# A projection started from raw, feature-major activations, and key projections moved into the feed-forward loop

## Chip, cores and metric

The kernel runs on one core of a Trainium2 chip. The metric is the device time of one execution in microseconds. PE is the matmul engine (TensorE), DVE the vector engine, ACT the scalar engine, POOL GpSimd and SP the sync engine, which issues most transfers here.

## What is computed

A network of three stages on 256 tokens of 1024 features, in float32: a block with three attention branches, then two layers with feed-forward parts and a second attention. The change touches the start of the first block and the feed-forward part between the two layers. Cut to that:

```
h = rmsnorm(x, g_mix)                 # x * rsqrt(mean(x*x) + EPS) * g
proj = h @ w_in                       # q, k, v of three branches, index scores, 3072 gate logits
m = rmsnorm(mem, g_mem)
mkv = m @ w_mem_kv                    # keys and values of the memory branch
gates = sigmoid(gate_logits + b_gate)
merged = gates[0]*(o_swa @ wp_swa) + gates[1]*(o_dsa @ wp_dsa) + gates[2]*(o_mem @ wp_mem)
x = x + merged @ w_out
...
kv = h @ kv_w                         # six slots of 4 groups x 64: 0, 1 compressed k and v,
                                      # 2, 3 selected k and v, 4, 5 window k and v
x = post_norm(x, swiglu(x, w1, w3, w2))
...                                   # attention with kv
```

The norm's factor is one number per token, so it can also be applied to a product's rows.

## The kernel before

Every large product is made in three matmuls (`mm3`): each operand is split into a high part, rounded to the matmul's format, and a low part, the rest; high times high, high times low and low times high are summed in PSUM. Activations lie feature-major: 8 tiles `k` of 128 features, each with 256 tokens, once as high part and once as low part (`x = (xh, xl)`). A product is made either with weights as the stationary operand (`up`: the result has features in partitions, 256 tokens as columns) or with activations as the stationary operand (`row`: tokens in partitions).

Weights come through one stream (`Stream`). Each piece of 256 columns is two loads of 512 KB on SP's queue into five rotating raw buffers. ACT casts a load to its high part (`wh`, L142) and DVE subtracts it to get the low part (`wl`, L149). `get` hands out the pieces in the order of the program, and `pump` prepares one ahead. A load waits until the subtraction of the load five places before it has freed its buffer.

The framework's planner orders the instructions of each engine by its own costs and priorities. Inside `manual(...)` the instructions of the named engines keep the order in which they are written, and others may be placed between them. Each engine works through its queue in order.

The first block, `mixers`, begins with `manual(DVE, ACT)`: x is loaded token-major in two row tiles, `rms_rows` makes statistics and the normalised rows, `norm_T` transposes them on PE in 16 pieces of 128x128, applies the gain `g_mix` on the way out of PSUM and splits the result. Gains and biases are loaded as rows (`vectors`) and transposed on PE too. `half` multiplies with the first 452 columns, by halves of the features and by row tiles, into two PSUM banks; L1353 copies the result to `PI`. Then follow two of twelve gate products (`gates`, two ACT copies each with the bias, L1388), rotary embedding of parts of PI on DVE (`rope`), transposes of it (`pair_T`, L597), the projection PQ (`rowproj`), index scores, the norm of memory by the same two functions, the projection PM, further projections by `up`, and three attentions, with the other ten gates and the top-k search (L1474, L1475) woven between them. `merge` applies the sigmoid.

`kv_ffn` runs two value slots by `row`, then slots 0 and 1 (`tokens`), then two key slots (`key`, L1031 and L1034, split by halves of 64 partitions), then a feed-forward part (`ff`) whose first chunk is made by `row` and transposed after swiglu (L535, L536, L497), the other chunks by `up`, with the compression of keys hooked in behind some chunks.

Of the kernel before, what the change touches and what calls it, by code (L numbers as in the profile page):

```python
# [23 lines left out]
F32 = mybir.dt.float32  # L24
# [3 lines left out]
OP = mybir.AluOpType  # L28
AX = mybir.AxisListType

S = 256
# [7 lines left out]
RAW = 5  # L39
LAST = 3  # L40
# [136 lines left out]
class Ker:  # L177
# [60 lines left out]
    def col(self, n, k):  # L238
        g, r = self.vec[n]
        return self.vt[g][:, r + k:r + k + 1]  # L240
# [6 lines left out]

    def vectors(self, names, q):

        nc, I = self.nc, self.I  # L250
        v = self.med([128, 128])
        r = 0
        g = len(self.vt)
        for n in names:
            ap = I[n]
            ap = ap.rearrange({1: "a -> a", 2: "a b -> (a b)", 3: "a b c -> (a b c)"}[len(ap.shape)])
            m = ap.shape[0] // 128
            q.dma_start(v[r:r + m], ap.rearrange("(r p) -> r p", p=128))
            self.vec[n] = (g, r)
            r += m  # L260
        t = self.cp.tile([128, r], F32, name=f"vt{g}")
        self.vt.append(t)

        def put():
            ps = self.bank()
            nc.tensor.transpose(ps[:, :r], v[:r], self.ident[:r, :r])
            nc.scalar.copy(t, ps[:, :r])

        return put
# [87 lines left out]
    def rms_rows(self, xs, ns, part=None, pin=False):  # L357

        nc = self.nc
        mvs = [self.stats(x, D, part, pin) for x in xs]  # L360
# [32 lines left out]

    def norm_T(self, n, t, g, b, x, act=False):

        nc = self.nc
        xh, xl = x
        ts = slice(t * 128, (t + 1) * 128)  # L400
        y = self.med([128, KT, 128])
        for h in range(4):
            ps = self.bank()
            for j in range(2):
                nc.tensor.transpose(ps[:, j * 128:(j + 1) * 128], n[:, (2 * h + j) * 128:(2 * h + j + 1) * 128],
                                    self.ident)
            for j in range(2):
                k = 2 * h + j
                p = ps[:, j * 128:(j + 1) * 128]
                sc = act or h % 2  # L410
                if b is None and sc:
                    nc.scalar.activation(y[:, k], p, AF.Copy, scale=g(k))  # L412
                elif b is None:
                    nc.vector.tensor_scalar(y[:, k], p, g(k), None, op0=OP.mult)
                elif sc:
                    nc.scalar.activation(y[:, k], p, AF.Identity, scale=g(k), bias=b(k))
                else:
                    nc.vector.tensor_scalar(y[:, k], p, g(k), b(k), op0=OP.mult, op1=OP.add)
        for h in range(4):
            ks = slice(2 * h, 2 * h + 2)  # L420
            end = self.split(xh[:, ks, ts], xl[:, ks, ts], y[:, ks])
        return end
# [576 lines left out]
    def kv_ffn(self, x, acc):  # L999
# [38 lines left out]
        def tokens(slot):  # L1038
# [5 lines left out]
            for a in range(2):  # L1044
                p = ps[:, a * S:(a + 1) * S]
                for e in range(2):
                    nc.scalar.copy(T[:64, 2 * a + e], p[half[e]])
                    nc.vector.tensor_copy(T[64:, 2 * a + e, :S - 1], p[half[e], 1:])
# [4 lines left out]
        for b in range(2):  # L1053
            key(b)
# [84 lines left out]
        f = self.ffn(x, 1, 0, acc, {1: keys, 2: lambda: windows(0), 3: lambda: windows(1), 4: compress})  # L1139
# [165 lines left out]
    def mixers(self, p):  # L1305
# [3 lines left out]
        sl = lambda t: slice(t * 128, (t + 1) * 128)  # L1309
        R = self.big([128, 2, D])  # L1310
        self.c, self.vec, self.vt = {}, {}, []
        nc.sync.dma_start(R[:, 0], I["x"][0, :128])
        names = ("ident", "tril_t", "rowok")
        self.load_cst(names, self.cp.tile([128, 257], F32, name="cst"))
        self.ident = self.cst("ident")
        put = [self.vectors(("g_mix", "g_mem"), nc.scalar)]
        nc.sync.dma_start(R[:, 1], I["x"][0, 128:])
        if not self.dry:
            for _ in range(4):
                W.load()  # L1320
# [3 lines left out]
        nr = [self.med([128, D]) for _ in range(2)]  # L1324
        put.append(self.vectors(("b_gate", "cmp_b1_2"), nc.sync))
        x = self.new_xT()
        gm = lambda k: self.col("g_mix", k)
# [3 lines left out]
        def half(ws, j, t):  # L1331
            for i in range(4):
                wh, wl = ws[i // 2]
                k = 4 * j + i
                self.mm3(ps[t][:, :452], x[0][:, k, sl(t)], x[1][:, k, sl(t)], wh[:, i % 2], wl[:, i % 2], k == 0, k == 7)

        with self.manual(mybir.EngineType.DVE, mybir.EngineType.Activation):
            put[0]()
            pw = [W.prep(), W.prep()]
            next(pw[0])  # L1340
            self.rms_rows([R[:, t] for t in range(2)], nr)
            self.norm_T(nr[0], 0, gm, None, x)
            next(pw[0], None)
            ws = W.get(w_in, 0, 4, 1024, 1476, False)
            half(ws, 0, 0)
            self.norm_T(nr[1], 1, gm, None, x)
            next(pw[1])
            next(pw[1], None)
            half(ws, 0, 1)
            ws = W.get(w_in, 512, 4, 1024, 1476, False)  # L1350
# [12 lines left out]
        def rowproj(w, c0, c1, x, P):  # L1363
# [29 lines left out]
        for f in put[1:]:  # L1393
            f()
# [194 lines left out]
```

## Time and profile before

| | us |
|---|---|
| median of 3 timed runs (lowest, highest) | 1489.09 (1487.06, 1489.27) |
| the profiled execution | 1489.02 |
| its span, from the first instruction to the last | 1487.2 |
| PE busy in the span | 1446.4 |
| DVE, ACT, POOL busy | 957.4, 736.1, 40.1 |

The profile is of one execution, and its time stands beside its span. An engine that is not the bottleneck may idle at no cost. Matmuls overlap, each beginning before the last has ended, so the distance between their starts says how fast PE goes, and a wait shorter than the overlap does not show as idle time.

### The profile page before, as it was taken

What the parts mean: (1) busy time and instruction counts of PE and PEld (TensorE: products, weight loads), DVE (VectorE), ACT (ScalarE), POOL (GpSimd) and SP (SyncE); (2) the same over time, 40 slices, a digit from 0 to 9 for tenths busy, and PEclk for the clock granted to TensorE, in tenths of its full rate; (3) what the DMA queues carried; (4) which work ended last, traced back from release to release, by engine and by line L of the source; (5) the groups of instructions that cost most, each with busy time, mean ns of one, the idle gap of its engine ahead of it and who ended that gap; (6) DMA issues with size and microseconds to landing.
All of it is one profiled execution on the core that took longest, in us unless ns stands there. A gap on an engine that the chain in (4) does not pass through costs nothing.

```text
span 1487.2 us, 25225 instructions
## 1 busy us (share of the span) xinstructions
PE 1446.4 (97%) x10093; PEld 1334.0 (90%) x10093; DVE 957.4 (64%) x1630; ACT 736.1 (49%) x1127; POOL 40.1 (3%) x49
## 2 busy tenths in 40 slices
PE   6899999999999999999999999999999999999997
PEld 6699898989999999889899999999999898899996
DVE  7884498555585445886785445866645778664544
ACT  5564565444354444554354444554544397354442
POOL 0000000000000000100010000100000121100001
PEclk9999999999999999999999999999999999999999
DMA  8443166655556665487556665466766452286650
GB/s 278 142 144 106 64 231 239 224 187 183 170 180 197 191 189 180 146 262 258 156 172 200 194 188 180 148 200 218 234 193 184 120 183 86 62 265 185 185 170 29
DMA packets 191714, 264.81 MB, mean 178 GB/s; under 512 B 11024, under 2 KB 159852, under 8 KB 191596
## 3 DMA queue, kind: packets, MB, share of 16 engines
q1 hardware_dynamic: 183068, 249.56, 52.9%
q10 hardware_dynamic: 8528, 13.64, 3.0%
q8 instruction: 79, 1.29, 0.3%
q14 instruction: 39, 0.32, 0.1%
HBM read 262.09 MB, written 1.07 MB: 177 GB/s over the span
## 4 chain that ended last, share of the span: by engine, by line
PE 82%; DVE 10%; ACT 3%; issue 2%; DMA 2%; POOL 0%; ACTq 0%; DVEq 0%; POOLq 0%
PE acc L311 21%; PE u L275 17%; PE u L276 17%; PE u L277 17%; DVE wl L149 3%; PE acc L276 2%; PE acc L695 2%; PE acc L277 2%; PE acc L275 2%; ACT wh L142 1%; DVE big L850 1%; DVE bst L379 1%; PE acc L681 1%; DVE big L828 1%; PE u L799 1%
## 5 line engine op out<-in xcount | busy, mean ns | idle before, releaser
L149 DVE TENSOR_TENSOR wl<-wr,wh 128x1024 fp32r<-128x1024 f32 (+3 forms) x488 | 573.2, 1184 | 419.0 <-ACT wh L142 406.6
L142 ACT CAST wh<-wr 128x1024 fp32r<-128x1024 f32 (+3 forms) x488 | 493.2, 1019 | 531.6 <-PE u L276 226.1
L275 PE MATMUL u<-big,wh 128*128 128x256 f32 x1960 | 552.5, 282 | 1.6 <-ACT med L412 1.1
L277 PE MATMUL u<-big,wl 128*128 128x256 f32 x1960 | 550.3, 281 | 0.0
L276 PE MATMUL u<-big,wh 128*128 128x256 f32 x1960 | 550.3, 281 | 0.0
L275 PEld LDWEIGHTS u<-big,wh 128*128 128x128 f32 x1960 | 369.9, 189 | 4.7 <-ACT med L412 1.3
L276 PEld LDWEIGHTS u<-big,wh 128*128 128x128 f32 x1960 | 369.0, 188 | 2.2
L277 PEld LDWEIGHTS u<-big,wl 128*128 128x128 f32 x1960 | 369.6, 189 | 0.0
L311 PE MATMUL acc<-wh,t 128*128 128x512 f32 x928 | 263.9, 395 | 0.0
L311 PEld LDWEIGHTS acc<-wh,t 128*128 128x128 f32 x928 | 169.7, 188 | 35.0
L311 PE MATMUL acc<-wl,t 128*128 128x512 f32 x464 | 145.6, 394 | 0.0
L311 PEld LDWEIGHTS acc<-wl,t 128*128 128x128 f32 x464 | 87.2, 188 | 20.6
L275 PE MATMUL u<-wh,big 128*128 128x256 f32 (+1 forms) x304 | 100.8, 331 | 0.5 <-ACT t L1429 0.5
L277 PE MATMUL u<-wh,big 128*128 128x256 f32 (+1 forms) x304 | 100.5, 330 | 0.0
L276 PE MATMUL u<-wl,big 128*128 128x256 f32 (+1 forms) x304 | 100.0, 329 | 0.0
L331 ACT CAST t<-t 128x512 fp32r<-128x512 f32 x66 | 41.0, 621 | 56.5 <-DVE t L536 25.3
L275 PEld LDWEIGHTS u<-wh,big 128*128 128x128 f32 x304 | 57.1, 188 | 6.9 <-ACT t L1429 0.9
L277 PEld LDWEIGHTS u<-wh,big 128*128 128x128 f32 x304 | 57.1, 188 | 5.5
L276 PEld LDWEIGHTS u<-wl,big 128*128 128x128 f32 x304 | 57.1, 188 | 5.2
L836 POOL TENSOR_TENSOR big<-big,med 128x256 f32<-128x256 f32 x24 | 23.2, 985 | 1389.2 <-ACT big L835 1355.7
L332 DVE TENSOR_TENSOR t<-t,t 128x512 fp32r<-128x512 f32 x66 | 45.4, 688 | 14.9 <-ACT t L331 14.9
L276 PE MATMUL acc<-wl,t 128*128 128x512 f32 (+1 forms) x168 | 53.8, 320 | 0.4 <-DVE wl L149 0.4
(256 smaller groups left out, 1356.5 us busy)
## 6 DMA issues: line engine op xcount, KB each, us to landing
wr<-in_ffn_w_dram SPq DMA_DIRECT2D x264, 512.0 KB, 4.5
wr<-in_w_in_dram SPq DMA_DIRECT2D x34, 512.0 KB, 4.3
wr<-in_w_mlp_in_dram SPq DMA_DIRECT2D x32, 512.0 KB, 4.6
wr<-in_w_mlp_out_dram SPq DMA_DIRECT2D x32, 512.0 KB, 3.8
wr<-in_sgu_w_in_dram SPq DMA_DIRECT2D x32, 512.0 KB, 5.3
wr<-in_sgu_w_out_dram SPq DMA_DIRECT2D x16, 512.0 KB, 6.4
wr<-in_kv_w_dram SPq DMA_DIRECT2D x12, 512.0 KB, 3.8
wr<-in_w_out_dram SPq DMA_DIRECT2D x8, 512.0 KB, 3.7
```

Of the source, the lines that this page charges most:

```text
L142: self.nc.scalar.copy(h, v)
L149: self.nc.vector.tensor_sub(l, v, h.bitcast(F32))
L275: mm(out, lh, rh, start=start, stop=False, **k)
L276: mm(out, lh, rl, start=False, stop=False, **k)
L277: mm(out, ll, rh, start=False, stop=stop, **k)
L311: mm(acc[t][n], a[:, k, ts], b[:, 0, n * 512:(n + 1) * 512], start=s, stop=e)
L331: self.nc.scalar.copy(h, x)
L332: return self.nc.vector.tensor_sub(l, x, h.bitcast(F32))
L379: b = nc.vector.bn_stats(st[:, 6 * i:6 * i + 6], x[:, c0:c1])
L681: nc.tensor.transpose(pt[:, c:c + 128], e[:, c:c + 128], self.ident)
L695: nc.tensor.matmul(out, PT[:, c:c + 128], v(b), start=b == 0, stop=b == nb - 1)
L836: nc.gpsimd.tensor_mul(x[:, cs], x[:, cs], gB[:, cs])
```

## The change

x and mem are prepared on the host feature-major as well (`xT`, `memT`), and the four small vectors as one table of 44 columns (`vecs`). The kernel multiplies these by the gain alone (`scale_T`, high part on ACT, low part on DVE) and uses them unnormalised; 1/rms is still made from the token-major x and mem (`rms_scale`), as a column `r` for products with tokens in partitions and, spread over 128 columns and transposed on PE, as a row `RB` for products with features in partitions. Products are multiplied by it when they leave PSUM: the gates and two memory products on DVE. The gates' bias is added with the sigmoid in `merge`. PE joins the engines whose order is kept as written at the start, and makes 14 matmuls on a tile of ones there. In `kv_ffn` the key projections move from before the feed-forward part to behind its chunks 4 and 6, the compression from 4 to 5, and the copies of keys and tokens out of PSUM take two groups at once.

```diff
-    def rms_rows(self, xs, ns, part=None, pin=False):
+    def rms_scale(self, xs, p, name, ones, pin=False):
...
-        for x, n, y in zip(xs, ns, self.rsqrt(nhs)):
-            for h in range(2):
-                hs = slice(h * 512, (h + 1) * 512)
-                nc.vector.tensor_scalar(n[:, hs], x[:, hs], y, None, op0=OP.mult)
+        r = p.tile([128, 2], F32, name=f"r{name}")
+        rb = p.tile([128, 2, 128], F32, name=f"rr{name}")
+        for t, y in enumerate(self.rsqrt(nhs)):
+            nc.vector.tensor_copy(r[:, t:t + 1], y)
+        for t in range(2):
+            nc.vector.tensor_scalar(rb[:, t], ones, r[:, t:t + 1], None, op0=OP.mult)
+        ps = self.bank()
+        for t in range(2):
+            nc.tensor.transpose(ps[:, t * 128:(t + 1) * 128], rb[:, t], self.ident)
+        B = p.tile([128, S], F32, name=f"rb{name}")
+        nc.scalar.copy(B, ps[:, :S])
+        return [r[:, t:t + 1] for t in range(2)], B[:, None, :].to_broadcast([128, 2, S])
+
+    def scale_T(self, raw, g, x, ks):
...
+        xh, xl = x
+        for k in ks:
+            nc.scalar.activation(xh[:, k], raw[:, k], AF.Copy, scale=self.col(g, k))
+        for k in ks:
+            nc.vector.scalar_tensor_tensor(xl[:, k], raw[:, k], self.col(g, k), xh[:, k].bitcast(F32), op0=OP.mult,
+                                           op1=OP.subtract)
...
-            for a in range(2):
-                p = ps[:, a * S:(a + 1) * S]
-                for e in range(2):
-                    g = 2 * a + e
-                    for d in range(2):
-                        h = self.kh[half[d], g, b]
-                        nc.scalar.copy(h, p[half[e]])
-                    q = self.kh[half[e], g, b].bitcast(F32)
-                    for d in range(2):
-                        nc.vector.tensor_sub(self.kl[half[d], g, b], p[half[e]], q)
+            p = ps.rearrange("p (a s) -> p a s", a=2)
+            for e in range(2):
+                for d in (e, 1 - e):
+                    nc.scalar.copy(self.kh[half[d], e::2, b], p[half[e]])
+                q = self.kh[half[e], e::2, b].bitcast(F32)
+                for d in range(2):
+                    nc.vector.tensor_sub(self.kl[half[d], e::2, b], p[half[e]], q)
...
-        for b in range(2):
-            key(b)
...
-        f = self.ffn(x, 1, 0, acc, {1: keys, 2: lambda: windows(0), 3: lambda: windows(1), 4: compress})
+        f = self.ffn(x, 1, 0, acc, {1: keys, 2: lambda: windows(0), 3: lambda: windows(1), 4: lambda: key(0), 5: compress, 6: lambda: key(1)})
...
+        nc.sync.dma_start(xr[:, :4], I["xT"][:, :4])
+        self.vt = self.cp.tile([128, 44], F32, name="vt")
+        nc.scalar.dma_start(self.vt, I["vecs"])
+        if not self.dry:
+            W.load()
+            W.load()
+        nc.sync.dma_start(xr[:, 4:], I["xT"][:, 4:])
...
+        for t in range(2):
+            nc.sync.dma_start(R[:, t], I["x"][0, t * 128:(t + 1) * 128])
...
+        with self.manual(mybir.EngineType.DVE, mybir.EngineType.Activation, mybir.EngineType.PE):
+            pw = self.bank()
+            for _ in range(14):
+                nc.tensor.matmul(pw[:, :128], one, one, start=True, stop=True)
+            for j in range(2):
+                pr = W.prep()
+                self.scale_T(xr, "g_mix", x, range(4 * j, 4 * j + 4))
+                next(pr)
+                next(pr, None)
+                ws = W.get(w_in, 512 * j, 4, 1024, 1476, False)
+                for i in range(2):
+                    for t in range(2):
+                        part(ws, j, i, t)
+            rx, RB = self.rms_scale([R[:, t] for t in range(2)], p, "x", one)
             for t in range(2):
-                half(ws, 1, t)
-                nc.scalar.copy(PI[:, t], ps[t][:, :452])
+                nc.scalar.activation(PI[:, t], ps[t][:, :452], AF.Copy, scale=rx[t])
         W.pump()
         mem = self.big([128, 2, D])
         nc.sync.dma_start(mem, I["mem"][0].rearrange("(t p) d -> p t d", p=128))
+        mr = self.big([128, KT, S])
+        nc.sync.dma_start(mr, I["memT"])
...
-                for f in range(2):
-                    nc.scalar.activation(gate[j // 4][:, 2 * (j % 4) + f], ps[:, f * S:(f + 1) * S], AF.Identity,
-                                         bias=self.col("b_gate", 2 * j + f))
+                nc.vector.tensor_mul(gate[j // 4][:, 2 * (j % 4):2 * (j % 4) + 2],
+                                     ps.rearrange("p (f s) -> p f s", f=2), RB)
...
-        for t in range(2):
-            self.norm_T(nm[t], t, lambda k: self.col("g_mem", k), None, m)
+        self.scale_T(mr, "g_mem", m, range(KT))
...
-                self.pin(nc.scalar.activation(g, g, AF.Sigmoid))
+                for f in range(2):
+                    e = gate[br][:, 2 * c + f]
+                    self.pin(nc.scalar.activation(e, e, AF.Sigmoid, bias=self.col("b_gate", 8 * br + 2 * c + f)))
```

## Rows read from the trace of the kernel before

**Rows 1.** The page's first part: busy time, share of the span, instructions.

```profile
span 1487.2 us, 25225 instructions
...
PE 1446.4 (97%) x10093; PEld 1334.0 (90%) x10093; DVE 957.4 (64%) x1630; ACT 736.1 (49%) x1127; POOL 40.1 (3%) x49
```

**Rows 2.** The timeline of PE: start, duration, line, operation, tiles, count.

```profile
27.60 0.36 PE L276 MATMUL acc<-wl,big 128*128 128x452 f32 x1
27.80 0.36 PE L277 MATMUL acc<-wh,big 128*128 128x452 f32 x1
...
33.26 0.28 PE L277 MATMUL u<-big,wl 128*128 128x256 f32 x1
33.38 0.28 PE L275 MATMUL u<-big,wh 128*128 128x256 f32 x1
```

**Rows 3.** The timeline of the head, all engines, 0 to 43 us.

```profile
4.53 1.35 DVE L379 BATCH_NORM_STATS2 bst<-big 128x6 f32<-128x512 f32 x3 [4.53 <-DMA big<-in_x_dram]
...
8.34 0.94 ACT L142 CAST wh<-wr 128x904 fp32r<-128x904 f32 x1 [1.58 <-DMA wr<-in_w_in_dram]
...
9.54 1.67 DVE L369 TENSOR_SCALAR med<-big,nwy 128x512 f32<-128x512 f32 x4
...
13.31 1.33 ACT L331 CAST big<-med 128x256 fp32r<-128x256 f32 x4
13.77 1.43 DVE L332 TENSOR_TENSOR big<-med,big 128x256 fp32r<-128x256 f32 x4 [1.51 <-ACT big L331]
...
13.96 0.73 PE L275 MATMUL acc<-wh,big 128*128 128x452 f32 x1
...
42.36 0.50 PE L275 MATMUL u<-wh,big 128*128 128x512 f32 x1
```

**Rows 4.** Groups of PE, 16.2 to 21 us: busy, mean ns | idle before.

```profile
L277 PE MATMUL acc<-wh,big 128*128 128x452 f32 x4 | 2.3, 580 | 0.0
```

**Rows 5.** The timeline of PE around the norm of memory.

```profile
67.64 0.39 PE L277 MATMUL u<-wh,big 128*128 128x512 f32 x1
...
73.03 0.38 PE L275 MATMUL u<-big,wh 128*128 128x256 f32 x1 [1.08 <-ACT med L412]
```

**Rows 6.** Waits of PE, 930 to 1080 us: in total, times, longest.

```profile
PE u L497 <- DVE t L536: 2.7, 1, 2.7
```

**Rows 7.** Stretches in and behind the key block: busy times, PEclk, DMA.

```profile
990.00:994.00 4.00, 2.59 (x12) 2.59 (x13) 3.15 (x4) 1.08 (x2) 0.00 (x0) 0.62 0.71 223
...
1003.00:1037.00 34.00, 34.00 (x241) 31.69 (x240) 23.15 (x23) 16.53 (x18) 0.00 (x0) 1.00 0.70 225
```

**Rows 8.** Groups of DVE, 21.7 to 42.3 us.

```profile
L149 DVE TENSOR_TENSOR wl<-wr,wh 128x1024 fp32r<-128x1024 f32 x8 | 9.7, 1223 | 3.1 <-ACT wh L142 3.1
L149 DVE TENSOR_TENSOR wl<-wr,wh 128x904 fp32r<-128x904 f32 x2 | 2.1, 1096 | 0.0
...
L379 DVE BATCH_NORM_STATS2 bst<-big 128x6 f32<-128x256 f32 x2 | 0.8, 422 | 0.0
```

**Rows 9.** Stretches of the first block: PE, PEld, DVE, ACT, POOL busy, PEclk, DMA.

```profile
10.00:20.00 10.00, 8.29 (x28) 6.89 (x29) 8.49 (x23) 7.59 (x21) 0.00 (x0) 1.00 0.96 338
21.70:42.30 20.60, 19.10 (x138) 18.26 (x136) 16.57 (x42) 12.43 (x23) 0.00 (x0) 1.00 0.74 233
56.00:95.00 39.00, 34.84 (x234) 30.47 (x234) 38.47 (x131) 21.79 (x46) 0.00 (x0) 1.00 0.47 142
95.00:190.00 95.00, 92.69 (x743) 86.14 (x742) 45.42 (x114) 52.97 (x132) 0.00 (x0) 1.00 0.32 96
```

**Rows 10.** Groups of DVE, 56 to 95 us.

```profile
L591 DVE TENSOR_TENSOR med<-med 128x512 f32<-128x512 f32 x1 | 0.7, 685 | 0.0
```

**Rows 11.** Waits of PE, 0 to 250 us.

```profile
PE u L597 <- ACT big L1388: 1.5, 1, 1.5
```

**Rows 12.** DMA issues: KB each, median us from issue to landing.

```profile
sink<-in_sinks_dram ACTq DMA_DIRECT2D x1, 4.0 KB, 6.5
```

**Rows 13.** Groups of the key block, 965 to 992 us.

```profile
L1034 DVE TENSOR_TENSOR big<-u,big 64x256 fp32r<-64x256 f32 x16 | 6.8, 422 | 2.0 <-ACT big L1031 1.7
...
L1031 ACT CAST big<-u 64x256 fp32r<-64x256 f32 x16 | 5.9, 368 | 4.2 <-DVE big L1034 4.0
```

More of the change, by code (lines that the diff above doesn't have):

```diff
@@ L39 @@
 RAW = 5
+VEC = {"g_mix": 0, "g_mem": 8, "b_gate": 16, "cmp_b1_2": 40}
 LAST = 3
@@ L246, in dump @@
             return True
[L248 to L269, printed above, removed]
     def mm3(self, out, lh, ll, rh, rl, start, stop, **k):
@@ L355, in rsqrt @@
         return [y for nh, y, a in ys]
-    def rms_rows(self, xs, ns, part=None, pin=False):
+    def rms_scale(self, xs, p, name, ones, pin=False):
         nc = self.nc
-        mvs = [self.stats(x, D, part, pin) for x in xs]
+        mvs = [self.stats(x, D, None, pin) for x in xs]
         nhs = [self.small(name="nh") for _ in xs]
@@ L392, in ln_rows @@
             nc.vector.tensor_scalar(x[:, c:c + 512], x[:, c:c + 512], mv[:, 0:1], y, op0=OP.subtract, op1=OP.mult)
[L394 to L422, printed above, removed]
     def weave(self, prev, A, B, nxt):
@@ L1043, in tokens @@
             T = self.med([128, 4, S])
[L1044 to L1048, printed above, removed]
+            p = ps.rearrange("p (a s) -> p a s", a=2)
+            for e in range(2):
+                nc.scalar.copy(T[:64, e::2], p[half[e]])
+                nc.vector.tensor_copy(T[64:, e::2, :S - 1], p[half[e], :, 1:])
             Ts.append(T)
@@ L1309, in mixers @@
         sl = lambda t: slice(t * 128, (t + 1) * 128)
+        self.c = {}
+        xr = self.big([128, KT, S])
         R = self.big([128, 2, D])
[L1311 to L1314, printed above, removed]
-        self.ident = self.cst("ident")
[L1316 to L1320, printed above, removed]
+        one = p.tile([128, 128], F32, name="one")
+        nc.vector.memset(one, 1.0)
+        nc.sync.dma_start(xr[:, :4], I["xT"][:, :4])
[5 more added lines that the diff above has]
+        nc.sync.dma_start(xr[:, 4:], I["xT"][:, 4:])
+        if not self.dry:
+            W.load()
+            W.load()
+        warm = self.small(8, "warm")
+        nc.scalar.copy(warm, one[:, :8])
+        self.load_cst(("ident", "tril_t", "rowok"), self.cp.tile([128, 257], F32, name="cst"))
+        self.ident = self.cst("ident")
+        for t in range(2):
+            nc.sync.dma_start(R[:, t], I["x"][0, t * 128:(t + 1) * 128])
         self.load_cst(("swa", "causal", "inv"), p.tile([128, 800], F32, name="cstp"))
@@ L1323, in mixers, with part @@
         nc.scalar.dma_start(pos, I["positions"].rearrange("o (t p) -> p (o t)", p=128))
-        nr = [self.med([128, D]) for _ in range(2)]
-        put.append(self.vectors(("b_gate", "cmp_b1_2"), nc.sync))
         x = self.new_xT()
-        gm = lambda k: self.col("g_mix", k)
         PI = self.med([128, 2, 452])
         ps = [self.bank("acc") for _ in range(2)]
[L1331 to L1350, printed above, removed]
+        def part(ws, j, i, t):
+            wh, wl = ws[i]
+            for e in range(2):
+                k = 4 * j + 2 * i + e
+                self.mm3(ps[t][:, :452], x[0][:, k, sl(t)], x[1][:, k, sl(t)], wh[:, e], wl[:, e], k == 0, k == 7)
+        with self.manual(mybir.EngineType.DVE, mybir.EngineType.Activation, mybir.EngineType.PE):
[12 more added lines that the diff above has]
+            rx, RB = self.rms_scale([R[:, t] for t in range(2)], p, "x", one)
             for t in range(2):
-                half(ws, 1, t)
-                nc.scalar.copy(PI[:, t], ps[t][:, :452])
+                nc.scalar.activation(PI[:, t], ps[t][:, :452], AF.Copy, scale=rx[t])
         W.pump()
@@ L1370, in rowproj @@
                 self.row(ws, *x, ps[:, :c1 - c0], t)
-                nc.scalar.copy(P[:, t], ps[:, :c1 - c0])
+                nc.scalar.activation(P[:, t], ps[:, :c1 - c0], AF.Copy, scale=r[t])
         gate = []
@@ L1415, in mixers @@
         PQ = self.med([128, 2, 512])
-        rowproj(w_in, 0, 512, x, PQ)
+        rowproj(w_in, 0, 512, x, PQ, rx)
         Rq = self.med([128, 2, 512])
@@ L1435, in mixers @@
             nc.vector.tensor_sub(isc[:, os_], isc[:, os_], self.cst("causal")[:, os_])
-        nm = [self.med([128, D]) for _ in range(2)]
-        self.rms_rows([mem[:, t] for t in range(2)], nm, None, True)
+        rm, MB = self.rms_scale([mem[:, t] for t in range(2)], p, "m", one, True)
         PM = self.med([128, 2, 512])
-        rowproj(w_in, 512, 1024, x, PM)
+        rowproj(w_in, 512, 1024, x, PM, rx)
         m = self.new_xT()
-        for t in range(2):
-            self.norm_T(nm[t], t, lambda k: self.col("g_mem", k), None, m)
+        self.scale_T(mr, "g_mem", m, range(KT))
         Rk = self.med([128, 2, 128])
@@ L1458, in mixers @@
         self.up(w, *m, ps)
-        nc.scalar.copy(flat(mkT), ps)
+        nc.vector.tensor_mul(mkT, ps.rearrange("p (f s) -> p f s", f=2), MB)
         ksT = p.tile([128, S], F32, name="ksT")
@@ L1584 @@
     arrays["consts"] = consts()[0]
+    vecs = [arrays.pop(n).reshape(-1, 128).T for n in VEC]
+    arrays["vecs"] = np.ascontiguousarray(np.concatenate(vecs, 1))
+    for n in ("x", "mem"):
+        arrays[n + "T"] = np.ascontiguousarray(arrays[n][0].T.reshape(KT, 128, S).transpose(1, 0, 2))
     nc = bacc.Bacc("TRN2", target_bir_lowering=False, num_devices=1, dynamic_dma_scratch_size=1024)
```

12 lines of the change are left out of this document (5 added, 7 removed).

## The prediction

> **What bounds the kernel now.** I read the page's shares first [rows 1]: PE is busy 97% of a span of 1487.2 us. The profiled execution took 1489.02 us, 1.8 us around the span, and the three timed runs have their median at 1489.09, so sums are made against 1489.0. A PE that is always busy can only be sped up by giving it fewer columns or by removing stretches in which it waits or runs at half speed. Busy time hides both, so I went through the stretches the diff touches in the timeline, by the distance from one matmul's start to the next. At full speed a 128x452 matmul follows the last after 0.20 us and a 128x256 one after 0.12 us [rows 2]. Against those paces three places lose time.
>
> *The head.* The first real matmul starts at 13.96 us, because x goes through statistics, normalisation, transposes, gains and the hi/lo split first [rows 3]. Until 21 us the 128x452 matmul lasts 580 ns [rows 4] against 360 to 370 later [rows 2]: the array runs at the lower of its two levels, 1.2 GHz, after a start with almost nothing to do. (The granted-clock column reads 1.00 there, as the trace holds no clock record before 21.5 us; the matmuls tell it.) The first matmul of the projection behind the head (PQ) starts at 42.36 us [rows 3]. Up to there PE has 48 matmuls of 452 columns (9.8 us at full pace), 96 of 256 (11.3) and 8 transposes (0.9): 22 us of work in 42.4.
>
> *The norm of memory.* The last matmul before it starts at 67.64 us, the first after it at 73.03 [rows 5]: 5.4 us, of which one pace (0.23) is work, and the rest is 16 transposes and waits.
>
> *The block with the key projections.* PE waits 2.7 us for swiglu's product [rows 6]; in 990 to 994 us the granted clock is 0.62 [rows 7], so after that idle stretch PE runs some 3 us at 1.2 GHz.
>
> **The change part by part.**
>
> *Head.* x arrives a second time, feature-major. Its first half is 512 KB, as the first row tile of x, which was there at 4.53 us [rows 3]. Then: four scalings on ACT, for which I take the casts of 128x256 (four in 1.33 us) → 5.9; the cast of the weight, 0.94 → 6.8; the subtraction on DVE, 1.10 [rows 3, 8] → 7.9 us. From there PE can go on. 48 matmuls take 9.8 us at full pace, 19 at half: to 18 or 27 us. The 14 warm-up matmuls cost PE nothing (it has no input before 6.8 us), and whether they raise the clock in time matters little, because DVE is later. From 4.9 us on it has 8 scaled subtractions of 128x256 (four splits took 1.43 us: 2.9), 4 subtractions for the weights (4.4), statistics and 1/rms of x (5.0, from 4.53 to 9.54 us now), four small copies (0.8) and 2 subtractions of 1.22 for the first gate [rows 3, 8]: 15.5 us, so the first gate runs at about 20 us. The change also puts two transposes of 1/rms into PE's written order behind the 48 matmuls; they wait for the copies of 1/rms on DVE, and the gates' matmuls queue behind them unless the planner puts those in front. Both come before DVE's 20 us, so this wait costs nothing of its own. Two gates: 96 matmuls, 11.3 → 31.3. DVE meanwhile has what it did between 21.7 and 42.3 us, 16.6 us, less 10 weight subtractions (11.8) and 0.8 of statistics [rows 8, 9]: 4.0 of rotary work, plus 2 multiplications for the gates (0.69 each, from a 128x512 product [rows 10]) and 4 weight subtractions (4.9): 10.3, hidden beside the gates. Eight transposes, 0.9 → 32.2. The wait of 1.5 us for the gates' old eviction on ACT [rows 11] falls away or moves to DVE. Data: by then about 9.7 MB must have come (x twice 2.1, mem twice 2.1, weights 5.0, constants 0.5); the stretch from 10 to 20 us moved 338 GB/s at a share of 0.96 [rows 9], which gives 28.7 us and, from 2 us on, 31. It is just covered. I add 2 us, since ACT, DVE and the transfers all come within 2 us of PE there: PQ starts at 34.3 us instead of 42.4, and I take **−8**. Bounds: −10 with nothing added; −3 if the 2 MB of mem and memT (6 us at that rate) go ahead of the gate's weights.
>
> The column vectors (176 bytes in each of 128 partitions) must be there before the first scaling. No transfer of theirs is in the trace; bounds are nothing (there with x, at 4.5 us) and the landing time of sink, 6.5 us [rows 12], which would give 7.2 us, 2.7 later. I take nothing: sink was issued behind a full queue, these go out first. The Trainium skill (DMA: Bandwidth & Descriptors, Specifications) says that transfers want 512 bytes or more in a piece to run at line rate, and below that are read, modified and written, which speaks against this table: by that the head would be worth nearer −6, and the sum 1474.5. sink, with pieces of 32 bytes, agrees with the slow end, but no row separates its size from its place in the queue.
>
> *Memory.* The gap of 5.4 less 0.23 us goes, and two transposes of 1/rms (0.2) come: −4.9. What stays are 8 scalings on ACT and 8 subtractions on DVE (2.9 us), needed only by the second projection behind it. DVE is busy 38.5 of 39 us from 56 to 95 [rows 9], but it loses there the normalising, the gains out of PSUM and the splits, and much of the rest is the top-k, which nothing needs until the last attention. **−4.5**; bounds −4.9, and −2 if the subtractions show.
>
> *Keys.* Today 16 casts and 16 subtractions of half the partitions stand between the tokens and the first product of the next block (5.9 us of ACT, 6.8 of DVE, each waiting for the other, 4.0 us on ACT alone [rows 13]), and swiglu's product queues behind them. Each key now makes 4 and 4 with twice the elements. They go beside chunks 4 and 6, where PE is the bound and DVE is busy 23 of 34 us and ACT 16.5 of 34 [rows 7]: two keys add 5.5 us of DVE to 34 us and more of PE, so they cost nothing there. If that cover were gone, 2 to 3 us would show. The keys' four weight loads move in the one stream of weights with their matmuls, so SP issues the same loads in another order, and PE does the same matmuls later. The tokens' copies, now halved in number, shorten the same queues. The wait of 2.7 goes, and with it the lower clock: some 3 us at half speed, 1.5. **−4.0** of 4.2; bounds −4.2 and −1.5 (the product still waits behind two weight subtractions, 2.4, and the clock falls less).
>
> *Evictions.* Rows scaled in the copy out of PSUM cost ACT what the copy did. Twelve gates move from ACT to DVE: 0.69 × 12 = 8.3 us of DVE, ten of them from 95 us on, where DVE is busy 45 of 95 us [rows 9]. Two small sigmoids instead of one: ACT has 42 of 95 us free. I take 0, between −1 (waits for ACT go) and +3.
>
> Sum: −8 −4.5 −4 = −16.5: **1472.5 us**. With all bounds at one end: −10 −4.9 −4.2 −1 = −20.1, 1469; −3 −2 −1.5 +3 = −3.5, 1485.5.
>
> **The rivals.**
>
> *The head's gain is given back.* DVE is full until 95 us [rows 9]. If PE arrives 8 us earlier at work that DVE feeds in order, top-k included, it waits there. For: 38.5 of 39. Against: DVE drops about 2.5 us of work ahead of 95 us and is idle 4 of 20.6 us in 21.7 to 42.3. Or the weights of the first gates queue behind mem and memT. Either way −3 in place of −8: about 1477.5, and 1480 where the norm of memory also only moves its wait.
>
> *The late vectors.* The first scaling waits until 7.2 us for the vectors [rows 12], and all behind it comes 2.7 us later: 1475. This is the case that the page on DMA speaks for.
>
> *The key wait stays,* because swiglu's product queues behind weight subtractions and not behind keys: 1475.
>
> *Slower: the gates' banks.* A gate's PSUM bank is now freed by DVE, in order, behind 1.22 us subtractions and attention's products. PE waited 1.5 us once for ACT in the same role [rows 11]. If each of the 12 gates waited so, and more, the gain would go at 16.5/12 = 1.4 us a gate; at 2 us each it is +7.5: 1496. For: DVE's full stretch holds several gates once the head is earlier. Against: four banks rotate, and DVE is half idle where ten gates run.
>
> *No change.* The planner that orders instructions by its own costs puts equal waits elsewhere: 1486 to 1492. Nothing in the rows speaks for it.
>
> **How the numbers follow.** Forecast 0.52 (1468 to 1477 its own range), head given back 0.20, late vectors 0.10, key wait stays 0.09, slower 0.05, no change 0.04. The predicted time is the likeliest case's, 1472.5. The range leaves out the last two cases and the far ends: 1466 to 1483. A measurement here tells 0.2%, 3 us, from no change. Faster 0.91, within 0.2% 0.04, slower 0.05.
>
> **What would show it.** First 452-column matmul near 7 us, and PQ's first at 34; last row projection and first of the next `up` a pace apart, with no transposes between; the wait for swiglu's product in the key block under 1 us and no clock below 1.00 there. Wrong if the first gate waits for weights until 25 us, if PE idles between 35 and 95 us for DVE by more than before, or if new waits for gate products appear after 95 us.

## The result, and the profile after

The changed kernel takes 1501.16 us (median of four, 1500.48 to 1503.1) against 1488.49: ratio 1.0087, 95% interval 1.0075 to 1.0100, **slower by 12.7 us** where 16.5 less was forecast. The profiled execution has a span of 1501.3 us. The page's shares, to be held against [rows 1]:

```profile
span 1501.3 us, 25158 instructions
...
PE 1458.9 (97%) x10091; PEld 1346.8 (90%) x10091; DVE 957.4 (64%) x1617; ACT 726.9 (48%) x1086; POOL 40.1 (3%) x49
```

PE has two instructions less than before and is busy 12.5 us longer; the share says 97% as it did. Busy shares hide both a wait that is made up elsewhere and a slower matmul, so the stretches have to be looked at one by one.

**Memory's 1/rms.** The timeline of PE around the place where [rows 5] showed the norm of memory:

```profile
52.98 1.21 PE L1391 MATMUL u<-kiT,qiT 64*128 64x256 f32 x7
65.01 0.66 PE L351 MATMUL u<-cst,rrm 128*128 128x128 f32 x2 [10.82 <-DVE rrm L348]
65.33 0.78 PE L252 MATMUL u<-wh,big 128*128 128x512 f32 x1
```

Behind the score matmuls of the index (16 from 51.80 us on; the first row shows the last seven) stand the two transposes of memory's 1/rms, and behind these the projection PM, 48 matmuls of 512 columns, which needs nothing of memory. PE stands still for 10.8 us, because the transposes wait for `rrm`. What DVE did in that time, from its timeline:

```profile
57.28 1.22 DVE L150 TENSOR_TENSOR wl<-wr,wh 128x1024 fp32r<-128x1024 f32 x1
...
58.75 1.01 DVE L374 BATCH_NORM_STATS2 bst<-big 128x6 f32<-128x512 f32 x2
...
61.00 0.23 DVE L1436 MAX8 m<-isc 128x8 f32<-128x128 f32 x1
...
64.20 0.41 DVE L1436 MAX8 m<-isc 128x8 f32<-128x256 f32 x1
...
64.59 0.47 DVE L348 TENSOR_SCALAR rrm<-one,rm 128x128 f32<-128x128 f32 x2
```

The statistics of memory come behind the rotary work and the index scores, and the small steps of 1/rms are interleaved with the top-k search. Busy time by stretch (PE, PEld, DVE, ACT, POOL, granted clock, DMA share, GB/s) shows what came of it, and of two other places:

```profile
21.95:25.20 3.25, 0.36 (x2) 0.00 (x0) 3.25 (x28) 2.38 (x3) 0.00 (x0) 1.00 1.05 400
...
53.90:65.00 11.10, 0.29 (x3) 0.02 (x1) 11.10 (x50) 1.58 (x5) 0.00 (x0) 0.62 0.44 135
65.00:70.20 5.20, 5.19 (x14) 4.15 (x15) 5.20 (x28) 0.37 (x1) 0.00 (x0) 0.50 0.01 2
...
1085.00:1088.00 3.00, 0.73 (x4) 0.33 (x2) 2.44 (x12) 2.60 (x5) 0.00 (x0) 0.90 0.74 251
1088.00:1094.00 6.00, 6.00 (x23) 5.42 (x23) 3.27 (x7) 1.28 (x2) 0.00 (x0) 0.50 0.58 174
```

DVE is busy all 11.1 us of the wait. After it PE runs at 1.2 GHz (0.50) until 70.2 us: 14 matmuls in 5.2 us.

**The head.** Rows of the timeline that answer to [rows 3]:

```profile
6.00 1.71 ACT L361 ACTIVATE big<-big,vt 128x256 fp32r<-128x256 f32 x4 [3.34 <-DMA vt<-in_vecs_dram]
...
8.59 0.60 PE L252 MATMUL acc<-wh,big 128*128 128x452 f32 x1 [2.10 <-ACT wh L143]
...
15.54 1.34 DVE L374 BATCH_NORM_STATS2 bst<-big 128x6 f32<-128x512 f32 x3
...
18.69 1.22 DVE L150 TENSOR_TENSOR wl<-wr,wh 128x1024 fp32r<-128x1024 f32 x1 [1.81 <-ACT wh L143]
...
19.98 1.28 DVE L374 BATCH_NORM_STATS2 bst<-big 128x6 f32<-128x512 f32 x3
...
25.23 0.33 PE L351 MATMUL u<-cst,rrx 128*128 128x128 f32 x1 [2.92 <-DVE rrx L348]
...
34.31 0.48 DVE L553 TENSOR_TENSOR med<-med,cosT 128x320 f32<-128x320 f32 x1
...
40.40 0.50 PE L252 MATMUL u<-wh,big 128*128 128x512 f32 x1
```

The first matmul comes 5.4 us earlier than before, PQ 2.0 us earlier (40.40 for 42.36). The 2.0 us are those of two profiles: over the experiments below, ten profiles with this head start PQ between 40.36 and 42.44 us, and four with the old head and the old norm of memory between 40.99 and 42.36. The statistics of x start at 15.54 us instead of 4.53. The token-major x is issued behind four weights and both halves of the feature-major one and lands 6.1 to 6.7 us after its issue at 8.67 and 9.41 us; DVE's last subtraction of those weights, ahead of them in its order, ends at 15.62 us. Which of the two held them is not to be told apart. The statistics of the second row tile come at 19.98 us, behind a subtraction for the first gate, whose cast on ACT waited until 17.61 us for its load. The gates stand behind the transposes of 1/rms until 25.23 us, and rotary work starts at 34.31.

**The key block.** The wait for swiglu's product [rows 6] is gone. Waits of PE from 930 to 1110 us:

```profile
PE u L1092 <- DVE med L1086: 2.3, 1, 2.3
```

It is in the compression at 1085 us, and the last row of the windows above shows six microseconds at half speed behind it. Five of six other profiles with the keys inside the loop have this wait too, 0.7 to 1.7 us long. ACT had waited 3.19 us for the weights of the second key:

```profile
1084.39 1.05 ACT L143 CAST wh<-wr 128x1024 fp32r<-128x1024 f32 x1 [3.19 <-DMA wr<-in_kv_w_dram]
```

These loads were issued at 1077.27 us; DVE's subtractions of them, and behind these the copies of the compression, came late.

### The profile page after: what moved, and what is told of

Read it like the earlier page. It is cut to its first block, busy times and chain, and to the rows that moved or that the text cites. A ratio compares the mean times of both kernels' runs of the same rounds, so it can differ in the third digit from the quotient of the medians.

```text
span 1501.3 us, 25158 instructions
## 1 busy us (share of the span) xinstructions
PE 1458.9 (97%) x10091; PEld 1346.8 (90%) x10091; DVE 957.4 (64%) x1617; ACT 726.9 (48%) x1086; POOL 40.1 (3%) x49
## 4 chain that ended last, share of the span: by engine, by line
PE 86%; DVE 9%; ACT 2%; DMA 2%; issue 1%; SPq 0%; DVEq 0%; ACTq 0%
PE acc L288 21%; PE u L252 18%; PE u L253 18%; PE u L254 18%; PE acc L660 2%; DVE wl L150 2%; PE acc L252 1%; PE acc L254 1%; PE acc L253 1%; DMA wr<-in_w_in_dram 1%; DVE bst L374 1%; ACT wh L143 1%; DVE big L815 1%; PE acc L646 1%; DVE big L793 1%
## 5 line engine op out<-in xcount | busy, mean ns | idle before, releaser
L150 DVE TENSOR_TENSOR wl<-wr,wh 128x1024 fp32r<-128x1024 f32 (+4 forms) x488 | 573.5, 1183 | 434.1 <-ACT wh L143 432.0
L143 ACT CAST wh<-wr 128x1024 fp32r<-128x1024 f32 (+4 forms) x488 | 492.9, 1019 | 547.0 <-PE u L253 236.7
L252 PE MATMUL acc<-wh,t 128*128 128x512 f32 (+1 forms) x168 | 54.1, 322 | 0.0
```

Of the source, the lines that this page charges most:

```text
L143: self.nc.scalar.copy(h, v)
L150: self.nc.vector.tensor_sub(l, v, h.bitcast(F32))
L252: mm(out, lh, rh, start=start, stop=False, **k)
```

## Experiments

Each ratio is to the kernel before, run on the same chip; differences are between medians. Executions of one kernel spread by up to 8 us here, so a difference below 2 us between two of them is not read.

### Memory's two transposes behind PM and qm

```diff
-        ps = self.bank()
-        for t in range(2):
-            nc.tensor.transpose(...)      # in rms_scale, at once
+        def spread(): ...                 # the same, called later
...
+        spread_m()
         w = W.get(wm, 0, KT, 0, 256)
```

> The changed kernel with one thing moved: the two transposes of memory's 1/rms on PE, and the copy of their bank on ACT, are issued behind the products PM and qm, just before the product that first needs them. The work on DVE that makes 1/rms stays where it was. Theory (PE stands in order behind these two transposes for 11.0 us at 53.8 us, and runs at the lower clock until 70.2 us after it): the wait goes and the lower clock with it, 13 us less than the 1501.2 of the changed kernel, so 1488, between 1485.5 and 1491. Rival 1 (DVE is the bound there and PE, freed here, waits for DVE at its next need, the two memory products or the attention): 1495 to 1501. Rival 2 (the loss lies in the added loads, 2 MB of x and memory a second time): within 2 us of 1501.

1489.67 us (ten executions, 1487.94 to 1495.0), ratio 1.0009 (0.9994 to 1.0024): **11.5 us less than the changed kernel**. The same stretches as above, of this kernel:

```profile
53.90:65.00 11.10, 10.44 (x49) 8.18 (x49) 10.87 (x40) 4.86 (x12) 0.00 (x0) 1.00 0.55 167
65.00:70.20 5.20, 5.20 (x34) 4.65 (x34) 5.20 (x17) 4.03 (x5) 0.00 (x0) 1.00 0.46 116
```

PE is busy 15.64 of 16.3 us at full clock, though DVE is as full as before. Two instructions, 0.66 us together, are at this place in PE's order the largest cause. Both rivals fall: PE waited for DVE at its next needs, up to 110 us, no longer than 0.3 us, and the added loads stayed.

The transposes of x's 1/rms were treated likewise, behind the matmuls of the first two gates:

> As the run with memory's transposes moved, and the two transposes of the 1/rms of x are also taken out of PE's written order at the start and stand behind the matmuls of the first two gates, whose results they scale. Theory (PE waited 3.1 us for them at 21.95 us and then ran 3.4 us at the lower clock, some 1.6 us lost): 4 to 5 us less than with memory's alone, about 1483.5, between 1481 and 1486. Rival (DVE reaches the first gate no earlier, so PE waits instead for rotary work or weights before PQ): within 1.5 us of the run with memory's alone.

1493.98 us (1486.89 to 1494.97), ratio 1.0026 (1.0010 to 1.0041). The ten executions cover much the same 7 to 8 us as those of the run above, so the time tells nothing; the profiles do. PQ starts at 40.65 us against 42.00, and the wait for `rrx` has become others. Waits of PE, 20 to 42 us:

```profile
PE u L565 <- DVE med L559: 3.0, 2, 2.4
PE u L565 <- ACT rbx L355: 1.2, 1, 1.2
```

The rival holds for the most part: the next thing in line is rotary work.

### Keys

```diff
+        for b in range(2):
+            key(b)                        # behind the tokens, as before
...
-{..., 4: lambda: key(0), 5: compress, 6: lambda: key(1)}
+{..., 4: compress}
```

> The changed kernel with the key projections and the compression back where the kernel before has them (keys behind the tokens, compression behind chunk 4); the wider copies out of PSUM stay. Theory (the move removed the wait for swiglu's product with its lower clock, 4.2 us, and brought a wait of 2.4 us in the compression at 1085 us with 6.8 us of lower clock behind it, 5.4 us together): 1500, between 1498 and 1502. Rival 1 (the wider copies alone already remove the wait, so nothing is lost by going back): 1495.5 to 1497. Rival 2 (the move is the cause of the slowdown): below 1492.

1499.72 us (1499.26 to 1500.41), 1.4 less than the changed kernel; the trace shows no wait above 1.2 us in the whole block, neither for swiglu's product nor in the compression. So the time fell where the theory had it, and the trace shows the first rival: the move had not removed the old wait, it only brought the new one. That the time meets the theory is luck. (In this profile PE waits 5.8 us for `rrx` in the head, where the changed kernel's waited 2.92, and PQ starts at 42.25 us, which hides part of the gain.) The wide copies were then put alone into the kernel before:

```diff
-            for a in range(2): ...        # one group at a time
+            p = ps.rearrange("p (a s) -> p a s", a=2)
+            for e in range(2):
+                for d in (e, 1 - e):
+                    nc.scalar.copy(self.kh[half[d], e::2, b], p[half[e]])
```

> The kernel before with one part of the change alone: the copies of tokens and keys out of PSUM take two groups at once (half as many, twice as wide); keys and compression stay at their old places, and the first block is the old one. Theory (the keys-back run showed no wait for swiglu's product although the keys were back at their place, so the wider copies, not the move, remove it, with the lower clock behind it): 4 us less than before, between 3 and 5.5. Rival (the wait went in that run only because the planner put the queue in another order): within 1.5 us of before.

1483.70 us (1482.86 to 1485.21), ratio **0.9969** (0.9957 to 0.9981), 4.6 us less. The group of DVE that answers to [rows 13], and the stretch around the old wait, in the kernel before and then in this run:

```profile
L1031 DVE TENSOR_TENSOR big<-u,big 64x512 fp32r<-64x512 f32 x8 | 5.5, 689 | 2.3 <-ACT big L1028 2.2
```

```profile
986.00:996.00 10.00, 7.28 (x52) 7.07 (x51) 6.85 (x9) 4.99 (x8) 0.00 (x0) 0.83 0.61 196
```

```profile
986.00:996.00 10.00, 9.99 (x86) 9.79 (x86) 6.90 (x8) 6.13 (x8) 0.00 (x0) 1.00 0.63 211
```

Half as many instructions, 1.3 us less of DVE, and PE is busy 9.99 of 10 us at full clock.

> The changed kernel with memory's two transposes behind the products PM and qm, and with keys and compression back at their old places. Theory (the move of keys costs a wait in the compression and lower clock behind it, 3.7 us in the profile with memory's transposes moved): 3 to 4 us less than memory's transposes alone (1489.7), so 1486, between 1483.5 and 1488. Rival (what is gained in that block is lost where the lower clock falls next): within 1.5 us of 1489.7.

1491.09 us (1488.96 to 1492.34), ratio 1.0018 (1.0010 to 1.0027), not the 1486 expected: beside moved transposes, the keys' place is worth nothing that the spread lets one see. The kernel before with the wide copies is 7.4 us faster, so the new first block costs more than the waits named so far.

> The run with memory's transposes moved and keys back, and in the head two more things: the transposes of the 1/rms of x stand behind the matmuls of the first two gates, and the tables of sine and cosine are written ahead of the statistics of x, so that rotary work on DVE waits only for the projection. Theory (PQ is held by rotary work, which started at 34.3 us because tables, statistics and weight subtractions share DVE): rotary work starts 2 to 4 us earlier and PQ with it, 2 to 4 us less than without, so 1483, between 1481 and 1486. Rival (DVE has as much to do as before and only changes its order): within 1.5 us of the run without these two.

1491.57 us (1488.27 to 1494.82): the rival. DVE got to the statistics of x later (30.70 us against 16.07; PE waits 5.1 us for `rrx`), and PQ starts at 43.77 us.

> The run with memory's transposes moved and keys back, without the 14 warm-up matmuls. Theory (the first projection starts when its weight's high part is there, at 8.5 us, and the first 21 us are held by loads and by DVE, so the level of the clock in them is worth little): within 1.5 us of the run with them. Rival (without them PE runs the 48 matmuls of the first projection at half speed to the end, and PQ comes later): 3 to 6 us more.

1491.58 us (1489.75 to 1493.91), 0.5 more, as the theory had it. PQ starts at 42.30 us against 41.52.

### Where 32 bytes lie

Matmuls of 256 columns in the feed-forward parts were found slower in every kernel with the new head, though the kernels make the same ones there. What was suspected is the place of tiles in memory: an ACT copy at the start writes a tile of 32 bytes a partition from the pool of small tiles, which keeps six buffers of it, and what is allocated behind lies 192 bytes further on.

```diff
-        warm = self.small(8, "warm")
+        warm = p.tile([128, 8], F32, name="warm")
```

> The changed kernel with one tile of 32 bytes a partition (the one that an early ACT copy writes) taken from the first block's own pool instead of the pool of small tiles that lives through the whole program. The instructions are the same; what moves back by 192 bytes a partition, to where the kernel before has it, is everything allocated behind that pool, three of the nine pairs of weight buffers among it. Theory (matmuls of 256 columns run 118.8 ns apart in the feed-forward parts of every kernel with the new first block against 116.8 to 118.2 in the two with the old one, and these addresses are what sets it): the pace returns to 116.8 to 118.2 and the time to 1497.5, between 1496 and 1499. Rival (the pace comes from something else, the order of the matmuls for one): within 1.5 us of 1501.2 and a pace of 118.8.

1494.72 us (1494.05 to 1495.7): **6.4 us less**, from the same instructions. Groups of PE by shape from 640 to 740 us (busy us, mean ns of one), the changed kernel and then this run:

```profile
L253 PE MATMUL u<-big,wh 128*128 128x256 f32 x128 | 36.1, 282 | 0.0
```

```profile
L253 PE MATMUL u<-big,wh 128*128 128x256 f32 x128 | 35.7, 279 | 0.0
```

Three nanoseconds in 280 are easy to pass over. From start to start, over the some 6800 records in the whole trace of one such matmul behind another (distances under 200 ns), the mean is 118.69 ns and then 117.65: 1.04 ns times 6800 is 7.1 us. The kernel before has 117.70. All nine profiles with the new head and the tile in the old pool lie between 118.68 and 118.73 ns, the seven with the old head or the moved tile between 117.65 and 117.74. Then the reverse, on the kernel before:

```diff
+        nc.vector.memset(self.small(8, "pad"), 0.0)      # second run: small(16, "pad")
```

> The kernel before with a pad of 32 bytes a partition in the pool of small tiles, six buffers of it as that pool gives: what is allocated behind moves by 192 bytes, to where the changed kernel has it. One more instruction on DVE, a memset of 8 columns. Theory (the addresses alone set the pace of 256-column matmuls): pace 118.7 instead of 117.7 ns and 6 us more than before, 1494.5, between 1492.5 and 1496. Rival (the pace depends on more than these addresses, and the old kernel does not feel them): within 1.5 us of 1488.5.

1495.56 us (1492.77 to 1496.67), ratio 1.0038 (1.0023 to 1.0053), 6.2 us more than before; the mean distance is 118.67 ns. The same group of the kernel before, and then of this run:

```profile
L276 PE MATMUL u<-big,wh 128*128 128x256 f32 x128 | 35.7, 279 | 0.0
```

```profile
L276 PE MATMUL u<-big,wh 128*128 128x256 f32 x128 | 36.1, 282 | 0.0
```

> The same with a pad of 64 bytes, so that everything behind moves by 384 bytes, a multiple of 128. Theory A (what counts is the place within 128 bytes): pace and time of the kernel before, 1488.5 within 1.5 us. Theory B (any move out of the old place costs): pace 118.7 and 1494.5, between 1492 and 1497. Estimates from the two known places only; no row speaks for either.

1490.71 us (1486.98 to 1492.33), ratio 1.0009 (0.9997 to 1.0020), mean distance 117.87 ns: much nearer theory A. Three places are not enough to say what of an address counts.

### Gates

```diff
-                nc.vector.tensor_mul(gate[...], ps.rearrange("p (f s) -> p f s", f=2), RB)
+                nc.scalar.copy(gate[...], ps.rearrange("p (f s) -> p f s", f=2))
```

> The changed kernel with the gates' products copied out of PSUM by ACT in one piece and not multiplied by 1/rms (this part of the computation is left out), so that DVE has 12 multiplications of 128x512 less, 8.3 us. Theory (the gates' banks are not what PE waits for, but DVE's list ahead of memory's 1/rms holds two of these multiplications): 1.4 us less at 54 us and up to 1 us in the attentions, 1499, between 1497 and 1501.5. Rival (gates' banks freed by DVE hold PE, the slower case of the forecast): below 1494.

1496.22 us (1494.58 to 1499.14), 4.9 less, twice the theory and short of the rival. The wait for memory's 1/rms stayed as it was; the gain lies behind 95 us. From 95 to 250 us the granted clock is 1.00 in both profiles, and PE idles 3.9 us of the 155 in the changed kernel and 1.0 in this run.

> The changed kernel with one sigmoid of 512 columns in place of two of 256 in each of the 12 places of the merge, as before the change; the gates' bias is left out for it. Theory (ACT is late with the casts for the output projection at the end of the merge because twice as many sigmoids stand before them): 2 us less than the changed kernel, 1499, between 1497.5 and 1500. Rival (the casts wait for their transfers and not for ACT): within 1 us of 1501.2.

1500.81 us (1500.1 to 1502.7): the rival, the sigmoids are not it. The one sigmoid was then tried where the other flaws are mended, and after it the gates on ACT:

> The run with memory's transposes moved and keys back (1491.1), with the tile of 32 bytes moved and with one sigmoid of 512 columns; the gates' bias is added by GpSimd behind the gates' product, so nothing is left out. Theory: 4 us less from the pace of the matmuls and 2 to 3 from the merge, 1484.5, between 1482.5 and 1487. Rival (either of the two does not hold, or GpSimd slows DVE in the attentions): 1487 to 1491.

1486.14 us (1481.33 to 1488.79), ratio 0.9984 (0.9974 to 0.9995); 5.0 less than the run that it builds on, where 6.6 was expected of the two together and the tile's place alone had brought 6.4.

> The changed kernel with memory's transposes behind PM and qm, keys at their old place, the tile of 32 bytes in the first block's pool, and the gates copied out by ACT with their bias as before the change, not multiplied by 1/rms (this factor is left out for the gates); one sigmoid of 512 columns. Theory (gates on DVE cost 5 us, as the run with ACT showed beside the changed kernel): 5 us less than the run in which GpSimd adds the bias (1486.1), so 1481, between 1479 and 1483.5. Rival (that gain was tied to the order that the memory wait made): 1484.5 to 1487.5.

1480.37 us (1479.03 to 1481.08), ratio 0.9938 (0.9923 to 0.9952): 5.8 us less by the gates on ACT, with GpSimd's additions gone as well. PE's waits for weights between 84 and 250 us (in total, times, longest), with DVE and then with ACT:

```profile
PE acc L288 <- DVE wl L150: 0.8, 1, 0.8
PE acc L288 <- ACT wh L143: 0.8, 1, 0.8
...
PE u L252 <- ACT wh L143: 0.7, 1, 0.7
...
PE u L254 <- DVE wl L150: 0.2, 1, 0.2
```

```profile
PE acc L253 <- DVE wl L150: 0.5, 3, 0.2
```

That is 2.5 us for casts and subtractions of weights with DVE, 0.5 with ACT; in the pair before it is 1.7 and none. A likely reading, not shown by a run of its own, is that the gates' products in DVE's queue hold up subtractions, and with them the loads that need the freed buffers. The waits of SP's queue do not settle it: those for DVE's subtractions fall from 56.0 to 41.6 us between 150 and 225 us, but waits for other work of DVE take their place, and in all they are 63 and 65 us. In this pair the granted clock goes with most of the rest, 0.96 from 84 to 180 us and 0.97 from 180 to 235 with DVE against 0.98 and 1.00 with ACT; whether the gates move the clock is open. It is not the PSUM banks: no wait of PE for a gate's product in that stretch exceeds 0.3 us in the changed kernel.

### Memory's part alone, and the change mended

The kernel before with the wide copies, memory's feature-major copy (`scale_T`, `rms_scale`) and the transposes behind PM and qm; head and gates are the old ones:

> The kernel before with two parts of the change alone: the wide copies of tokens and keys at their old places (1483.7 by themselves), and memory multiplied unnormalised from the feature-major copy, with the two transposes of 1/rms behind the products PM and qm. The head and the gates are those of the kernel before. Theory (the forecast's term for memory, -4.5, holds where the transposes do not stand in front of PM): 1479.2, between 1477.5 and 1481.5. Rival (PE waits for DVE or for memory's products elsewhere, or the further 1 MB of loads delays the weights): 1482 to 1485.

**1481.59 us** (1481.14 to 1482.19), ratio **0.9956** (0.9941 to 0.9970): faster than both kernels, with nothing left out. Memory's part brings 2.1 us over the wide copies, short of the 4.5, although the gap of [rows 5] is closed to a pace:

```profile
68.09 0.39 PE L277 MATMUL u<-wh,big 128*128 128x512 f32 x1
68.32 0.28 PE L275 MATMUL u<-big,wh 128*128 128x256 f32 x1
```

Its PQ starts at 42.81 us, 0.45 later than in the kernel before and 1.3 later than in the profile with the wide copies alone (41.47), so part of what the norm of memory gives is gone before it.

> The changed kernel, whole, with two things mended: memory's transposes behind PM and qm, and the tile of 32 bytes in the first block's pool. Theory (the wait with its clock is worth 11.5 us, the addresses 6.4, and they add): 1483.5, between 1481.5 and 1487. Rival (they do not add, because PE at the faster pace waits more for DVE or for weights): 1487 to 1491.

1486.74 us (1484.15 to 1491.54), ratio 0.9983 (0.9971 to 0.9994): the two mends take 14.4 us off, of 17.9 if they added fully.

## Why the prediction was wrong

| term of the sum | forecast | by the runs |
|---|---|---|
| Head | -8 | -1.2, or -2.1 with each held against the kernel before on its own chip: about the least that is read here (from the run with memory's part on the old head, 1481.59, to the one with the new head and gates on ACT, 1480.37) |
| Memory | -4.5 | -2.1, and +11.5 for the wait before PM |
| Keys | -4.0 | -4.6 by the wide copies; +1.4 by the move, and -1.4 where memory's transposes are moved, neither of which is read |
| Evictions | 0 | +4.9 to +5.8 for the gates on DVE |
| addresses | not in the sum | +6.2 to +6.4 |
| sum (with +1.4 for the move) | -16.5 | +16 to +17; measured +12.7 |

The parts overlap by some 4 us. The run with two mends shows 3.5 of it. A likely reading is that part of what is won early is lost again later: that run's profile has the lower clock from 148 to 154 us, where the changed kernel's has not.

**Memory** is the step that failed and turned the sign. It counted the two new transposes as work (0.2 us) and not as a wait. For x the forecast asked what stands behind such transposes in PE's order; for memory it did not, although the diff makes them inside `rms_scale`, ahead of `rowproj` for PM, where `norm_T` had stood behind it. The row that it needed was there: DVE busy 38.5 of 39 us [rows 9]. That DVE "loses" work there was true and no help, as the chain of 1/rms stands late in its list. A sign of being wrong that the forecast named, PE idle between 35 and 95 us for DVE by more than before, is the one that came.

**Head.** The first matmul near 7 us came at 8.59, PQ not at 34.3 but at 40.40. The wrong step is that both waits come "before DVE's 20 us", a time got by adding up DVE's work without a wait. The sum of the work came out: DVE is busy 15.46 us between 4.90 and 25.23 us, for 15.5 forecast. Left out were 4.9 us in which it stands still: until 6.54 us for the table and ACT's first scaling, and then 3.2 us for casts of weights, 1.8 of them in front of the second row tile's statistics. "This wait costs nothing of its own" was wrong too: 2.92 us here and up to 5.8 in another profile of the same head, and the rotary work counted as hidden beside the gates waits for 1/rms as well. The rival *the head's gain is given back* is nearest to what happened.

**The late vectors** fell: ACT starts scaling at 6.00 us, 1.5 behind the forecast's 4.5 and 1.2 ahead of this rival's 7.2. The table takes 5.0 us from issue to landing, where a half of the feature-major x takes 4.9 (medians of the DMA view). The Trainium skill (DMA: Bandwidth & Descriptors, Specifications) has pieces below 512 bytes slower than line rate. The delay that this rival drew from it is not in the trace, which does not test the sentence itself: the table's 22 KB in 176-byte pieces took as long as the 512 KB issued with it, and no run has the table in longer pieces.

**Keys** had the right size by luck, for a wrong reason: the copies' count, not their place. The move was costed at nothing for DVE and ACT beside PE, and its loads as "another order"; in the compression, with a DMA share of 1.05 from 1080 to 1085 us, the trace has a new wait of 2.3 us and the lower clock behind it. With the keys at their old place neither is there; what the move costs in time stays open, as the two differences in the table go opposite ways.

**Evictions.** The rival *the gates' banks* had the right engine at the wrong place. The gates on DVE cost 4.9 to 5.8 us for all twelve, under the 16.5 at which they would have decided alone, and not by a bank that PE waits for. Up to 2 us are waits for weights; the path of the rest is not shown.

**The addresses** no step could have given: no row of the kernel before shows a second level of that pace.

## What to carry to other kernels

When a change adds even one small instruction to the engine that is the bound, ask what is queued behind it and when its input is ready in the producer's list; 0.66 us of transposes cost 11.5 us, and writing them two products later gave that back. Test the parts of a bundled change alone: here one was worth 4.6 us, two others about 2 each or less, and three things cost 5 to 11.5 each. After any edit compare the mean time of the commonest matmul in a stretch that the edit does not touch, before looking for waits.

## What the runs showed of the hardware

The place of tiles in the on-chip memory (SBUF) changes the pace of 256-column matmuls: 192 bytes further on, one lasts 282 ns instead of 279 in the stretch from 640 to 740 us, which is 6.2 us on the kernel before and 6.4 on the changed one; 384 bytes cost at most 3 us (interval of the ratio 0.9997 to 1.0020). Which operand it is, and why, was not tried.

The granted clock falls to 1.2 GHz not only behind long idle stretches: in the run with two mends it is 0.77 from 145 to 160 us, and 0.50 from 148 to 154. Before it fell, PE worked on the small matmuls of the attentions from 143 us on, and its longest wait was 0.51 us; in the whole stretch it is busy 14.45 of 15 us. In the profiles of the kernel before and of the changed kernel the clock is 1.00 there. Executions of one kernel differ in their mean clock, and the time goes with it: of the run with memory's transposes moved, the five below 1489 us have 0.993 to 0.996, the four above 1492 have 0.990 to 0.992.

```profile
145.00:160.00 15.00, 14.45 (x86) 13.17 (x86) 5.64 (x20) 5.99 (x17) 0.00 (x0) 0.77 0.17 61
```
